# A 90-degree rotation of an 8192 x 8192 matrix: a third output buffer, five chunks fewer, and the last tile kept whole

## The chip, the core and the metric

The kernel runs on one core of one Trainium2 chip. The metric is the time of one execution in microseconds (us). Each kernel was executed several times, in turn with the kernel before on the same chip. All the times below are of runs that the records call fast.

The engines in the profiles are these. PE is the matrix engine, and PEld is its loading of the stationary operand. DVE is VectorE, ACT is ScalarE, and POOL is GpSimd. SP is the engine whose queue issues the loads. Every transfer runs on the 16 DMA engines of the core.

## The reference

```python
def setup_inputs():
    return {"x": np.random.randn(8192, 8192).astype(np.float32), "k": 1}

def reference(x, k):
    return np.rot90(x, k)          # out[i, j] = x[j, 8191 - i]
```

All 268.44 MB are read once and written once. The rest is rearrangement.

## The kernel before

The matrix is cut into 16 macro tiles of 1024 rows x 4096 columns. A macro tile is loaded as eight row tiles of 128 x 4096 (2 MiB each, one load each). VectorE copies each row tile into eight "chunks" of 128 x 512 and reverses the columns within each block of 128. PE then transposes the 128 x 128 blocks into PSUM, ScalarE copies the PSUM tile to an output buffer, and one store of 2 MiB writes four blocks of output rows. A macro tile has eight such outputs, and each needs a block from every one of its row tiles.

```python
    a_pool = ctx.enter_context(tc.tile_pool(name="a_pool", bufs=2))    # loads, 2 MiB each
    r_pool = ctx.enter_context(tc.tile_pool(name="r_pool", bufs=68))   # chunks; 64 hold a macro tile
    o_pool = ctx.enter_context(tc.tile_pool(name="o_pool", bufs=2))    # outputs, 2 MiB each
    psum_pool = ...  bufs=2
    ...
            for h in range(0, G, PW):                 # an output has two PSUM tiles
                pt = psum_pool.tile([P, FP], mybir.dt.float32, tag="ps")
                for w in range(PW):                   # column by column ...
                    g = g0 + h + w
                    for t in range(rt):               # ... through all row tiles
                        nc.tensor.transpose(..., chunks[t, g * P // CH][:, g % (CH // P), :], ident)
                nc.scalar.copy(o[:, G - PW - h : G - h, :], ps)
                ...
                    nc.scalar.dma_start(out=dst, in_=o[:, G - done : G - done + S, :])
    ...
    *most, before_last, last = tiles       # the last macro tile is split into 4 + 4 row tiles
    for m in most:
        store(*m, load(*m), False)
    c1 = load(*before_last)
    c2 = load(*last)
    store(*before_last, c1, True)
    store(*last, c2, True)                 # the very last output is stored in two halves
```

Of the kernel before, what the change touches and what calls it, by code (L numbers as in the profile page):

```python
# [2 lines left out]

# [5 lines left out]

P = 128  # L10




R = 1024
RT = R // P
LAST = [4, 4]
W = 4096
CH = 512
F = 4096  # L20
FP = 2048


def whole_reads(nc):






    for fn in nc.m.functions:
        for block in fn.blocks:
            for n, ins in enumerate(block.instructions):
                if not isinstance(ins, mybir.InstDMACopy):
                    continue
                src = ins.ins[0]
                ap = [list(d) for d in src.ap]
                if len(ap) == 3 and ap[2][0] == 1 and ap[1][0] == ap[2][1]:
                    ap = [ap[0], [1, 1], [1, ap[1][1] * ap[2][1]]]
                    block.instructions[n] = copy.replace(  # L40
                        ins,
                        ins=[copy.replace(src, ap=ap)],
                        ant_dge_precooked=False,
                    )


def macro_tiles(N, M):

    tiles = [(r0, RT, c0) for r0 in range(0, N, R) for c0 in range(0, M, W)]
    r0, _, c0 = tiles.pop()  # L50
    for n in LAST:
        tiles.append((r0, n, c0))
        r0 += n * P
    return tiles


@with_exitstack
def kernel(
    ctx: ExitStack,
    tc: tile.TileContext,  # L60
    x: bass.AP,
    k: bass.AP,
    out: bass.AP,
):
    nc = tc.nc
    assert k == 1, f"only k=1 supported, got {k}"
    nc.at_finalize(whole_reads)

    N, M = x.shape
    dt = x.dtype  # L70

    consts = ctx.enter_context(tc.tile_pool(name="consts", bufs=1))
    ident = consts.tile([P, P], dt)
    make_identity(nc, ident)

    a_pool = ctx.enter_context(tc.tile_pool(name="a_pool", bufs=2))
    r_pool = ctx.enter_context(tc.tile_pool(name="r_pool", bufs=68))
    o_pool = ctx.enter_context(tc.tile_pool(name="o_pool", bufs=2))
    psum_pool = ctx.enter_context(
        tc.tile_pool(name="psum", bufs=2, space=bass.MemoryType.PSUM)  # L80
    )

    loads = 0

    def load(r0, rt, c0):





        nonlocal loads
        chunks = {}
        for t in range(rt):


            if loads < RT and loads % 4 >= 2:
                a = o_pool.tile([P, W], dt, tag="o")
            else:
                a = a_pool.tile([P, W], dt, tag="a")
            loads += 1  # L100
            nc.sync.dma_start(
                out=a[:], in_=x[r0 + t * P : r0 + (t + 1) * P, c0 : c0 + W]
            )
            for j in range(W // CH):
                ar = r_pool.tile([P, CH // P, P], dt, tag="ar")
                nc.vector.tensor_copy(  # L106
                    out=ar[:],
                    in_=a[:, j * CH : (j + 1) * CH].rearrange(
                        "r (b m) -> r b m", m=P
                    )[:, :, ::-1],  # L110
                )
                chunks[t, j] = ar
        return chunks

    def store(r0, rt, c0, chunks, end):





        rows = rt * P
        PW = 1
        while 2 * PW * rows <= FP:
            PW *= 2
        G = PW
        while 2 * G * rows <= F:
            G *= 2
        for i, g0 in enumerate(range(0, W // P, G)):
            if end and i % 2 == 0:
                ot = a_pool.tile([P, F], dt, tag="a")  # L130
            else:
                ot = o_pool.tile([P, F], dt, tag="o")
            o = ot[:, : G * rows].rearrange("m (g f) -> m g f", g=G)

            S = PW if end and r0 + rows == N and g0 + G == W // P else G
            for h in range(0, G, PW):
                pt = psum_pool.tile([P, FP], mybir.dt.float32, tag="ps")
                ps = pt[:, : PW * rows].rearrange("m (g f) -> m g f", g=PW)
                for w in range(PW):
                    g = g0 + h + w  # L140
                    for t in range(rt):
                        nc.tensor.transpose(  # L142
                            ps[:, PW - 1 - w, t * P : (t + 1) * P],
                            chunks[t, g * P // CH][:, g % (CH // P), :],
                            ident,
                        )
                nc.scalar.copy(o[:, G - PW - h : G - h, :], ps)  # L147

                done = h + PW
                if done % S == 0:  # L150
                    top = M - c0 - (g0 + done) * P
                    dst = out[top : top + S * P, r0 : r0 + rows].rearrange(
                        "(g m) f -> m g f", g=S
                    )
                    nc.scalar.dma_start(  # L155
                        out=dst, in_=o[:, G - done : G - done + S, :]
                    )

    tiles = macro_tiles(N, M)
    *most, before_last, last = tiles  # L160
    for m in most:
        store(*m, load(*m), False)

    c1 = load(*before_last)
    c2 = load(*last)
    store(*before_last, c1, True)
    store(*last, c2, True)


# [1 line left out]
_INS = ['x', 'k']  # L171
_OUTS = [((8192, 8192), 'float32')]

_NUMBERS = {'k': 1}


# [26 lines left out]
```

## Time and profile before

| | before |
|---|---|
| median, lowest, highest of the first 3 runs | 1267.77, 1267.59, 1268.42 us |
| span of the profiled execution | 1266.0 us |
| bytes read + written | 268.44 + 268.44 MB, 424 GB/s over the span |
| busy: PE, ACT, DVE | 55%, 37%, 28% |
| DMA share in the 40 slices | 9 tenths in 39 of them |

The DMA row and the GB/s row decide here. The DMA engines are at nine tenths or more in nearly every slice, so the other engines only have to keep them fed. The lines themselves stand in the prediction. The column "DMA share" of the stage tables is the mean over 16 engines.

### The profile page before, as it was taken

What the parts mean: (1) busy time and instruction counts of PE and PEld (TensorE: products, weight loads), DVE (VectorE), ACT (ScalarE), POOL (GpSimd) and SP (SyncE); (2) the same over time, 40 slices, a digit from 0 to 9 for tenths busy, and PEclk for the clock granted to TensorE, in tenths of its full rate; (3) what the DMA queues carried; (4) which work ended last, traced back from release to release, by engine and by line L of the source; (5) the groups of instructions that cost most, each with busy time, mean ns of one, the idle gap of its engine ahead of it and who ended that gap; (6) DMA issues with size and microseconds to landing.
All of it is one profiled execution on the core that took longest, in us unless ns stands there. A gap on an engine that the chain in (4) does not pass through costs nothing.

```text
span 1266.0 us, 10386 instructions
## 1 busy us (share of the span) xinstructions
PE 700.4 (55%) x4096; PEld 660.8 (52%) x4096; DVE 354.9 (28%) x1024; ACT 467.3 (37%) x257; POOL 0.7 (0%) x6
## 2 busy tenths in 40 slices
PE   1456455665655555555556546565464665656573
PEld 0355455554545455554555445464464654556573
DVE  4422322232222322233222322233222332223210
ACT  0333334333433334333433334333433334333364
POOL 0000000000000000000000000000000000000000
PEclk9986777777678777787777877778777667777687
DMA  9999999999999999999999999999999999999998
GB/s 398 416 431 429 429 428 429 430 427 430 427 429 429 429 429 430 428 429 428 430 428 428 429 429 427 427 429 426 430 429 427 414 428 430 426 427 428 428 393 370
DMA packets 37057, 537.55 MB, mean 425 GB/s; under 512 B 4112, under 2 KB 4112, under 8 KB 4112
## 3 DMA queue, kind: packets, MB, share of 16 engines
q10 hardware_dynamic: 18576, 268.44, 50.0%
q1 hardware_dynamic: 18432, 268.44, 49.9%
q8 instruction: 32, 0.52, 0.2%
q14 instruction: 17, 0.14, 0.0%
HBM read 268.44 MB, written 268.44 MB: 424 GB/s over the span
## 4 chain that ended last, share of the span: by engine, by line
DMA 78%; ACT 19%; issue 1%; DVE 1%; ACTq 0%; PE 0%; DVEq 0%
DMA out_dram<-ot 74%; ACT ot L147 19%; DMA a<-in_x_dram 3%; DVE ar L106 1%; ACTq L155 0%; PE pt L142 0%; ACTq L147 0%; DVEq L106 0%
## 5 line engine op out<-in xcount | busy, mean ns | idle before, releaser
L142 PE MATMUL pt<-ident,ar 128*128 128x128 f32 x4096 | 700.4, 350 | 548.3 <-ACT ot L147 465.9
L142 PEld LDWEIGHTS pt<-ident,ar 128*128 128x128 f32 x4096 | 660.8, 187 | 587.7 <-ACT ot L147 496.4
L147 ACT COPY ot<-pt 128x2048 f32<-128x2048 f32 x256 | 466.0, 1869 | 742.6 <-DMA out_dram<-ot 729.5
L106 DVE COPY ar<-a 128x512 f32<-128x512 f32 x1024 | 354.9, 420 | 865.8 <-DMA a<-in_x_dram 811.4
L147 ACT ACT_TABLE_LOAD x1 | 1.3, 1283 | 41.1 <-DVE ar L106 41.1
masks.py:199 POOL TENSOR_SCALAR_AFFINE_SELECT ident<-ident 128x128 f32<-128x128 f32 x1 | 0.3, 294 | 0.1
masks.py:197 POOL MEMSET ident<- 128x128 f32 x1 | 0.2, 205 | 0.3 <-POOLq L184 0.3
L184 POOL MEMSET const-bfloat16-1.0<- 128x1 bf16 x1 | 0.1, 102 | 0.0
L184 POOL MEMSET const-uint8-127<- 128x1 uint8 x1 | 0.1, 102 | 0.0
L184 POOL MEMSET const-float32-0.0<- 128x1 f32 x1 | 0.1, 99 | 0.2 <-issue 0.2
L184 POOL MEMSET const-float32-1.0<- 128x1 f32 x1 | 0.1, 99 | 0.0
## 6 DMA issues: line engine op xcount, KB each, us to landing
a<-in_x_dram SPq DMA_DIRECT2D x128, 2048.0 KB, 16.8
out_dram<-ot ACTq DMA_DIRECT2D x127, 2048.0 KB, 15.9
out_dram<-ot ACTq DMA_DIRECT2D x2, 1024.0 KB, 13.7
```

The lines of the kernel that those rows point to most:

```text
L106: nc.vector.tensor_copy(out=ar[:], in_=a[:, j * CH : (j + 1) * CH].rearrange("r (b m) -> r b m", m=P)[:, :, ::-1],)
L142: nc.tensor.transpose(ps[:, PW - 1 - w, t * P : (t + 1) * P], chunks[t, g * P // CH][:, g % (CH // P), :], ident,)
L147: nc.scalar.copy(o[:, G - PW - h : G - h, :], ps)
L184: nc = _bacc.Bacc("TRN2", target_bir_lowering=False, num_devices=1)
```

## The change

The change is meant to keep the store queue filled. A third output buffer lets three stores be in flight; to make room for it, the chunks go from 68 to 63. The first output of each macro tile is transposed row tile by row tile, so that its chunks come free as the rows arrive. The last macro tile is no longer split. Its first output, like its last one, is stored in two halves. One line of the change is left out below: at the start the first eight loads are spread over five buffers (`loads % 5`) where they were spread over four, since the new output buffer is lent to them too.

```diff
-LAST = [4, 4]
...
-    tiles = [(r0, RT, c0) for r0 in range(0, N, R) for c0 in range(0, M, W)]
-    r0, _, c0 = tiles.pop()
-    for n in LAST:
-        tiles.append((r0, n, c0))
-        r0 += n * P
-    return tiles
+    return [(r0, RT, c0) for r0 in range(0, N, R) for c0 in range(0, M, W)]
...
-    r_pool = ctx.enter_context(tc.tile_pool(name="r_pool", bufs=68))
-    o_pool = ctx.enter_context(tc.tile_pool(name="o_pool", bufs=2))
+    r_pool = ctx.enter_context(tc.tile_pool(name="r_pool", bufs=63))
+    o_pool = ctx.enter_context(tc.tile_pool(name="o_pool", bufs=3))
...
-            S = PW if end and r0 + rows == N and g0 + G == W // P else G
+            S = PW if end and (i == 0 or g0 + G == W // P) else G
...
+            if i == 0 and (rt == RT or r0 + rows < N):
+                for h in range(G // PW):
+                    psum_tile(h)
+                for t in range(rt):
+                    transposes(t, range(G))
             for h in range(0, G, PW):
-                (transposes column by column, as above)
+                if h // PW not in ps:
+                    psum_tile(h // PW)
+                    (transposes column by column, as before)
...
-    c1 = load(*before_last)
-    c2 = load(*last)
-    store(*before_last, c1, True)
-    store(*last, c2, True)
+    for m in tiles:
+        store(*m, load(*m), m == tiles[-1])
```

## The prediction

> **What bounds the kernel now.** I read four views in this order: the page's slices, the page's groups, a table of stages, and the timeline at the two ends. The page first.
>
> ```profile
> PEclk9986777777678777787777877778777667777687
> DMA  9999999999999999999999999999999999999998
> GB/s 398 416 431 429 429 428 429 430 427 430 427 429 429 429 429 430 428 429 428 430 428 428 429 429 427 427 429 426 430 429 427 414 428 430 426 427 428 428 393 370
> HBM read 268.44 MB, written 268.44 MB: 424 GB/s over the span
> L142 PE MATMUL pt<-ident,ar 128*128 128x128 f32 x4096 | 700.4, 350 | 548.3 <-ACT ot L147 465.9
> L147 ACT COPY ot<-pt 128x2048 f32<-128x2048 f32 x256 | 466.0, 1869 | 742.6 <-DMA out_dram<-ot 729.5
> L106 DVE COPY ar<-a 128x512 f32<-128x512 f32 x1024 | 354.9, 420 | 865.8 <-DMA a<-in_x_dram 811.4
> ```
>
> The DMA row is 9 in every slice but the last. The rate is 426 to 431 GB/s in nearly all slices, and lower only in the first two, in one late slice (414) and in the last two. ScalarE waits 729.5 of its 742.6 idle us for stores, VectorE 811.4 of 865.8 for loads, and PE for ScalarE. So everything waits in the end for the DMA engines, and every byte must go through them: the output needs all of the input, 268.44 MB each way. The chain of waits says the same: 74% stores, 19% ScalarE copies, 3% loads. Its 19% should not be read as a fifth of the span to be won: a store lands, its buffer is refilled in 3.64 us and stored again, but the other buffer's store and two loads run beside that copy.
>
> What one transfer costs is best read where nothing but loads runs, in the timeline of the first 50 us:
>
> ```profile
> 12.99 2.77 DVE L106 COPY ar<-a 128x512 f32<-128x512 f32 x8 [2.12 <-DMA a<-in_x_dram]
> 17.88 2.77 DVE L106 COPY ar<-a 128x512 f32<-128x512 f32 x8 [2.12 <-DMA a<-in_x_dram]
> 22.79 2.77 DVE L106 COPY ar<-a 128x512 f32<-128x512 f32 x8 [2.13 <-DMA a<-in_x_dram]
> ```
>
> VectorE starts on each load as it lands, so loads of 2 MiB land 4.90 us apart: 2.097 MB / 4.90 us = 428 GB/s, the same rate as in the mixed middle. There are 128 loads and 128 stores' worth of data, so the data alone takes 256 x 4.90 = 1253 us (1254 if the page's mean middle rate of 428 is used). The time of 1267.8 is thus 14 us above what the engines need, 1.1%, and that is the whole purse for a change that moves no byte less. The table of stages says where it lies:
>
> ```profile
> core 0: us, PE busy (x) PEld busy (x) DVE busy (x) ACT busy (x) POOL busy (x), PEclk, DMA share, GB/s
> 0.00:3.00 3.00, 0.00 (x0) 0.00 (x0) 0.00 (x0) 0.00 (x0) 0.70 (x6) 1.00 0.44 104
> 3.00:76.00 73.00, 25.23 (x141) 21.31 (x142) 30.50 (x88) 15.93 (x9) 0.00 (x0) 0.93 1.01 424
> 76.00:1204.00 1128.00, 637.45 (x3670) 604.13 (x3669) 318.87 (x920) 417.01 (x230) 0.00 (x0) 0.74 1.01 428
> 1204.00:1222.00 18.00, 14.54 (x91) 14.02 (x92) 5.55 (x16) 9.41 (x6) 0.00 (x0) 0.74 0.88 371
> 1222.00:1262.00 40.00, 23.21 (x200) 21.31 (x198) 0.00 (x0) 24.91 (x14) 0.00 (x0) 0.86 1.00 418
> 1262.00:1266.00 4.00, 0.00 (x0) 0.00 (x0) 0.00 (x0) 0.00 (x0) 0.00 (x0) 0.50 0.11 47
> ```
>
> The last two columns are what counts. I turn each rate into time lost against 428: start 3 x (1 - 104/428) = 2.3 us; loads and first stores 73 x (1 - 424/428) = 0.7; middle 0; a hole near the end 18 x (1 - 371/428) = 2.4; the stores alone 40 x (1 - 418/428) = 0.9; after the last byte 4 x (1 - 47/428) = 3.6. The sum is 9.9; the rest of the 14 us is 1.8 us by which the timed run is longer than the profiled span, the DMA of instructions (0.66 MB, 1.5 us), and rounding.
>
> **The hole**, seen closely in the timeline and in 2-us windows:
>
> ```profile
> 1211.80 3.63 ACT L147 COPY ot<-pt 128x2048 f32<-128x2048 f32 x2 [6.21 <-DMA out_dram<-ot]
> 1215.46 0.55 ACTq L155 DMA_DIRECT2D out_dram<-ot  x1
> 1220.82 0.55 ACTq L155 DMA_DIRECT2D out_dram<-ot  x1
> ...
> 1214.00:1216.00 2.00, 2.00 (x11) 2.00 (x11) 0.00 (x0) 1.43 (x1) 0.00 (x0) 0.50 0.29 123
> 1220.00:1222.00 2.00, 2.00 (x21) 1.96 (x20) 0.76 (x3) 1.33 (x2) 0.00 (x0) 1.00 0.66 279
> ```
>
> No load is left to issue after 1201 us. The last store of the second-last macro tile waits until a buffer is stored (1211.7), is copied in 3.63 us and issued at 1215.46. Meanwhile only one store and the rest of the last load are in the queues; they run dry at about 1214 (share 0.29). The next store is issued 5.4 us later, while one store is 4.9 us of work, and there is a second hole (0.66).
>
> **What the Trainium skill says.** (1) "DMA: Bandwidth & Descriptors", Where 436 GB/s comes from: the 16 ports give 435.2 GB/s. The trace's 428 in the middle is 98% of that, so it agrees, and leaves no room for a faster middle. (2) The same page, Queues, rings and completion order: each DMA engine takes turns between the queue rows that have work, packet by packet. The trace agrees: the two queues took 50.0% and 49.9% of the engines' time. It follows that a deeper store queue doesn't take bandwidth from loads, it only keeps its own turn filled. (3) The same page, Latency and other measured facts: a fixed cost of about 2 us per DMA, mostly the receipt from memory. The first load landed 7.33 us after issue and carries 4.90 us of data, so 2.4 us here; this is why a single outstanding store isn't enough at the end.
>
> **The change, part by part.**
>
> Work on the engines: unchanged. 4096 transposes, 1024 reversals, 256 copies, 128 loads stay; stores go from 127 of 2048 KB and 2 halves to 126 and 4 halves. One more issue of 0.55 us on ScalarE's queue: nothing.
>
> Third output buffer: a copy waits for the store three back, not two back. Stores in flight rise from 15.9/9.8 = 1.6 to about 2.6 (9.8 us is the time for one load and one store). In the middle the engines are full already: gain 0.
>
> 63 chunks, 68 before: a chunk is 128x512 floats; 64 hold a macro tile. With 68, after output i of a tile is transposed, 8i + 12 chunks of the next can be filled; row tile i needs 8i + 8, so it is complete after output i. With 63 it is 8i + 7, so it is complete only after output i + 1. But with three buffers output i + 1 is transposed once output i is evicted, which waits for store i - 3; before, output i was transposed once output i - 1 was evicted, which waited for the same store i - 3. Loads keep their place against the stores that have landed: cost 0. The 64th chunk needs one chunk of its own macro tile free. That is what the row-by-row first output is for: row tile 0's four transposes release its first chunk before row tile 7 is reversed, so it can't deadlock. After the last row tile only 4 transposes are left to do in place of up to 18 or so, and the first store goes out about 1.5 us earlier (49.65 us before). At the start this is worth nothing, since two more loads fill the engines at that moment.
>
> The end: the last load should land with the rest of one store and two whole stores queued, some 2.6 x 4.9 = 12 us of work. Until the first new half store is issued it takes a reversal 0.42, four transposes about 0.7, a copy 1.87: 3.0 us, and some 0.6 us of issue. 12 against 3.6: no hole. After that an output costs ScalarE 4.3 us (issue to issue 1225.13 to 1229.46) against 4.9 us of transfer, and five buffers alternate: it stays filled. Gain: 2.4 us.
>
> The last macro tile whole: its stores write rows of 1024 floats instead of 512. Whether the 418 GB/s of the store-only stretch comes from the short rows or from stores alone the trace doesn't say; I take half of the 0.9 us: 0.5. Against that, the store-only stretch is longer by about one store.
>
> Start 2.3 and after the last byte 3.6: untouched. Sum: 2.4 + 0.5 = 2.9 us, so 1267.8 - 2.9 = **1264.9 us**.
>
> **Rivals.** (a) The deeper queue speeds the middle. For: the page's rate dips, such as 414 in one slice. Against: share 1.01 and 98% of the ceiling; even 430 in place of 428 over 1128 us would give only 5 us more: about 1260. (b) The chunk limit becomes the wait. For: VectorE already waited seven times, 54.4 us in total, for PE to release chunks, and there are now five chunks fewer. If loads lose step at each of 16 macro tiles for 2 us with the stores drained, it is +30 us, 1295. Against: the counting above, and three stores to fill in. (c) PSUM: the first output now holds both PSUM tiles while row tiles arrive. But PE and ScalarE have nothing else to do then; it would need all outputs of the tile before to be held, and they are evicted already. Zero, 1265. (d) The hole merely moves: 1268.
>
> **Range and chances.** Low end: all of hole and store-only stretch recovered and a little in the middle, 1261.5. High end: nothing recovered, 1268. Two per cent faster is 1242, below the 1253 of data alone: impossible at this rate, so 0.01 for a surprise in the rate. Slower by 2% is rival (b): 0.01.
>
> **What would show it.** Right: middle at 428 again; no 2-us window between the last load and the last store under 0.9 of DMA share; stores landing in about 25 us in place of 15.9; the store-only stretch about 50 us. Wrong: VectorE's waits for PE growing by tens of us with DMA share under 0.95 in the middle (b); a middle rate above 430 (a); a hole at the last load with a DMA share of 0.3 as now (d).

## The result

| | before | changed |
|---|---|---|
| median, lowest, highest of 6 runs each | 1268.09, 1267.59, 1269.21 us | 1269.88, 1269.54, 1270.63 us |
| ratio to before, 95% interval | | 1.0014, 1.0002 to 1.0027 |
| span of the profiled execution | 1266.0 us | 1268.8 us |

A ratio here is the mean time of one kernel's fast runs over the mean of the other's of the same rounds, so it is not quite the ratio of the medians. The changed kernel is within 2% of the old one, as forecast, but it is 1.8 us slower where 2.9 us faster was predicted.

The page of the changed kernel: the rate in 40 slices, ScalarE's copies with what they waited for, and the stores with their median time from issue to landing.

```profile
GB/s 398 427 429 430 429 428 429 429 429 429 428 429 427 430 429 428 428 429 429 429 428 429 430 420 430 429 429 427 424 430 428 417 429 426 427 428 424 429 338 381
L158 ACT COPY ot<-pt 128x2048 f32<-128x2048 f32 x256 | 466.4, 1869 | 762.3 <-DMA out_dram<-ot 506.5
out_dram<-ot ACTq DMA_DIRECT2D x126, 2048.0 KB, 25.5
```

Stores now take 25.5 us from issue to landing, where they took 15.9: three are in flight, as intended. ScalarE waits less for stores (506.5 us, before 729.5). The middle has the rate that it had. The slice before the last fell from 393 to 338 GB/s; the last has 381 in place of 370.

The stages of the changed kernel, cut as in the prediction (columns as there; the last two are DMA share and GB/s):

```profile
3.00:76.00 73.00, 30.16 (x177) 25.96 (x178) 30.62 (x88) 19.46 (x11) 0.00 (x0) 0.96 1.01 429
76.00:1204.00 1128.00, 625.40 (x3665) 587.76 (x3663) 319.14 (x920) 417.25 (x230) 0.00 (x0) 0.74 1.01 428
1204.00:1222.00 18.00, 8.13 (x36) 7.19 (x37) 5.55 (x16) 4.45 (x3) 0.00 (x0) 0.59 0.85 359
1222.00:1262.00 40.00, 28.18 (x222) 26.33 (x220) 0.00 (x0) 26.48 (x15) 0.00 (x0) 0.88 0.92 385
```

The middle is 428 GB/s in both. By this mean, all of the loss is after 1204 us: 359 in place of 371, and 385 in place of 418.

The end in the timeline of the changed kernel (start, duration, engine, work, count, and in brackets the idle time before it and what ended it):

```profile
1202.12 3.63 ACT L158 COPY ot<-pt 128x2048 f32<-128x2048 f32 x2 [6.19 <-DMA out_dram<-ot]
1205.78 0.55 ACTq L166 DMA_DIRECT2D out_dram<-ot  x1
...
1218.09 2.77 DVE L100 COPY ar<-a 128x512 f32<-128x512 f32 x8 [7.03 <-DMA a<-in_x_dram]
...
1219.30 3.63 ACT L158 COPY ot<-pt 128x2048 f32<-128x2048 f32 x2 [13.55 <-PE pt L137]
1221.19 2.31 ACTq L166 DMA_DIRECT2D out_dram<-ot  x2
...
1221.22 8.32 PE L137 MATMUL pt<-ident,ar 128*128 128x128 f32 x48 [1.53 <-ACT ot L158]
...
1227.84 1.87 ACT L158 COPY ot<-pt 128x2048 f32<-128x2048 f32 x1 [1.04 <-PE pt L137]
1229.73 0.55 ACTq L166 DMA_DIRECT2D out_dram<-ot  x1
```

The same stretch in windows of 2 us of the changed kernel:

```profile
1218.00:1220.00 2.00, 1.12 (x4) 0.72 (x4) 1.91 (x6) 0.70 (x1) 0.00 (x0) 0.50 0.50 213
1220.00:1222.00 2.00, 0.78 (x4) 0.78 (x5) 0.86 (x3) 2.00 (x2) 0.00 (x0) 0.50 0.14 57
...
1228.00:1230.00 2.00, 1.79 (x17) 1.55 (x15) 0.00 (x0) 1.70 (x1) 0.00 (x0) 1.00 0.08 29
1230.00:1232.00 2.00, 1.72 (x16) 1.48 (x14) 0.00 (x0) 1.60 (x1) 0.00 (x0) 1.00 0.61 262
```

**The first hole.** The last store of the tile before the last is issued at 1205.78. ScalarE then waits 13.55 us for PE, because the first output of a whole last tile needs its eighth row tile, which lands at 1218.09. In those 12.3 us the DMA engines can move 12.3 x 428 GB/s = 5.3 MB, or 2.5 transfers. From 1218 us on the rate falls to 213 and then 57 GB/s: for most of the DMA engines nothing is left to do.

**The second hole.** The first output is stored in two halves at 1221.19, which is 4.9 us of transfer. The next store follows only at 1229.73. PE was idle from 1210 to 1218.6 us, and its granted clock, the third column from the right, is 0.50. The 48 transposes that start at 1221.22 (32 for the second output, 16 for the third) take 8.32 us, and the copy waits for them.

### The profile page after: what moved, and what is told of

Its sections match the earlier page's. It is cut to its first block, busy times and chain, and to the rows that moved or that the text cites. A ratio compares the mean times of both kernels' runs of the same rounds, so it can differ in the third digit from the quotient of the medians.

```text
span 1268.8 us, 10386 instructions
## 1 busy us (share of the span) xinstructions
PE 691.9 (55%) x4096; PEld 647.2 (51%) x4096; DVE 355.3 (28%) x1024; ACT 467.7 (37%) x257; POOL 0.7 (0%) x6
## 4 chain that ended last, share of the span: by engine, by line
DMA 80%; DVE 11%; ACT 4%; PE 3%; issue 1%; ACTq 0%; DVEq 0%; SPq 0%
DMA a<-in_x_dram 69%; DMA out_dram<-ot 11%; DVE ar L100 11%; ACT ot L158 4%; PE pt L137 3%; ACTq L166 0%; DVEq L100 0%; SPq L95 0%; ACTq L158 0%
## 5 line engine op out<-in xcount | busy, mean ns | idle before, releaser
L137 PE MATMUL pt<-ident,ar 128*128 128x128 f32 x4096 | 691.9, 347 | 561.4 <-ACT ot L158 401.5
L137 PEld LDWEIGHTS pt<-ident,ar 128*128 128x128 f32 x4096 | 647.2, 184 | 605.8 <-ACT ot L158 438.2
L158 ACT COPY ot<-pt 128x2048 f32<-128x2048 f32 x256 | 466.4, 1869 | 762.3 <-DMA out_dram<-ot 506.5
## 6 DMA issues: line engine op xcount, KB each, us to landing
out_dram<-ot ACTq DMA_DIRECT2D x126, 2048.0 KB, 25.5
```

The costliest lines, as they stand in the source:

```text
L137: nc.tensor.transpose(ps[w // PW][:, PW - 1 - w % PW, t * P : (t + 1) * P], chunks[t, g * P // CH][:, g % (CH // P), :], ident,)
L158: nc.scalar.copy(o[:, G - PW - h : G - h, :], ps[h // PW])
```

## The experiments

### A second way of reading the end: the last landing

The first experiments gave results that the mean DMA share could not explain, so I read one more thing from the traces. Each transfer marks its landing 16 times, once for each DMA engine. The Trainium skill says so ("DMA: Bandwidth & Descriptors", Why a DMA increments its semaphore by 16 and not by 1), and the trace agrees: the kernel before has 257 transfers and 4112 landing records, 16 x 257. A transfer is complete with the sixteenth. The sixteen are far apart. In the kernel before, first and last mark of one transfer are 2.2 us apart at the start (median of the first 32 transfers), 7.1 us in the fourth 32, and 8.2 to 8.4 in the fifth to seventh. So some DMA engines lag behind others by more than a transfer and a half (8.2 / 4.9). The next table, worked out from these records, has the time of the last mark for the end of eight runs.

```
us from the span's start; the last of 16 marks
                 last    last store    outputs of the last macro tile (a halved one: its second half)        from the 2nd   first-to-last
                 load    of the tile     1       2       3       4       5       6       7       8            column to      mark of the
                         before                                                                               output 8       last store
before          1217.9    1224.9      1229.9  1235.0  1240.1  1245.4  1250.1  1255.1  1260.0  1265.0         40.1           2.7
changed         1218.0    1224.8      1229.9  1236.5  1241.4  1246.4  1253.2  1258.0  1263.0  1267.8         43.0           2.0
e1_split_tail   1216.8    1224.0      1228.9  1233.9  1238.9  1243.9  1248.9  1253.9  1258.8  1263.8         39.8           7.0
e2_whole_tail.. 1218.3    1225.1      1231.0  1237.7  1242.6  1247.5  1253.6  1258.5  1263.4  1268.3         43.2           2.0
e4_warm_pe      1219.4    1225.5      1230.6  1235.6  1240.7  1246.8  1251.7  1256.6  1261.5  1266.4         40.9           1.8
r1_after        1219.7    1225.7      1230.8  1238.1  1243.0  1248.0  1254.8  1259.7  1264.6  1269.5         43.8           1.9
r2_warm         1217.5    1224.8      1229.7  1234.6  1240.3  1244.9  1249.8  1254.7  1259.7  1264.6         39.8           1.9
r3_split        1218.0    1225.0      1230.1  1235.1  1240.1  1245.2  1250.1  1255.1  1260.0  1265.0         40.0           7.1
```

Two things can be read here. In the kernel before, stores complete every 5 us from 1224.9 to the end, straight through the "hole" that the mean showed there. And the last store of the tile before the last completes at the same time before and after the change (1224.9 and 1224.8): nothing up to there made a difference, not even the first hole of the changed kernel, since output 1 also completes at 1229.9 in both. A caution: each row is one execution. Those of e1_split_tail, e4_warm_pe and r2_warm are the fastest of their kernels (r2_warm's took 1267.37 us, its others 1269.20 to 1269.86), that of the changed kernel is its slowest. So the distances within a row say more than the times at which it ends.

### e1_split_tail: the old end with the rest of the change

```diff
-    return [(r0, RT, c0) for r0 in range(0, N, R) for c0 in range(0, M, W)]
+    (split of the last macro tile into 4 + 4, both loaded before either is stored, as before)
-            S = PW if end and (i == 0 or g0 + G == W // P) else G
+            S = PW if end and r0 + rows == N and g0 + G == W // P else G
```

> The changed kernel with only its end put back: last macro tile split 4+4, both halves loaded before either is stored, only the very last output in halves. Theory A (the whole last macro tile has nothing to store between the last store of the tile before it and its own eighth row tile, so the store queue runs dry while the last load is under way): no 2-us window under 0.9 of DMA share between 1204 us and the end, and about 1265 us, 3 us under the kernel before and 5 under the changed one. Rival B (the third output buffer or the chunk limit costs the time): stays at about 1270 us, with the middle under 428 GB/s.

Measured: 1267.69 us median of 5 (1266.55 to 1268.63), ratio to before 1.0001 (0.9987 to 1.0014). Three profiles of one 30-us stretch follow: before, changed, and this one.

```profile
1210.00:1240.00 30.00, 24.22 (x197) 22.42 (x195) 3.65 (x11) 23.11 (x13) 0.00 (x0) 0.94 0.93 389
```

```profile
1210.00:1240.00 30.00, 18.78 (x133) 17.33 (x132) 3.83 (x12) 15.60 (x9) 0.00 (x0) 0.77 0.80 334
```

```profile
1210.00:1240.00 30.00, 22.78 (x197) 20.98 (x194) 2.77 (x8) 22.48 (x13) 0.00 (x0) 1.00 1.01 421
```

The hole is gone, as theory A (in the expectation above) said: 421 GB/s where the kernel before has 389. By the mean that is 30 x (421 - 389)/428 = 2.2 us won. Yet the time is that of the kernel before, not 1265. What the engines gained on average they lost at the end of the same run:

```profile
1256.00:1258.00 2.00, 0.00 (x0) 0.00 (x0) 0.00 (x0) 0.00 (x0) 0.00 (x0) 0.50 0.70 291
1258.00:1260.00 2.00, 0.00 (x0) 0.00 (x0) 0.00 (x0) 0.00 (x0) 0.00 (x0) 0.50 0.47 197
```

The DMA share falls step by step, as one engine after another runs out of work, while the last goes on to 1263.8: the marks of the last store are 7.0 us apart (2.7 before). That is why I formed theory D: the end is set by the DMA engine that lags most, and a hole in the mean makes the leading engines wait, not the lagging one. Theory A holds for the difference to the changed kernel. Rival B (third buffer or chunk limit) falls, since both are in this run. So is the new start.

### e2_whole_tail_only: the new end with the rest as before

The edit is the reverse: the kernel before with only the hunks of the end (no split, first and last output in halves).

> The kernel before (two output buffers, 68 chunks, transposes column by column) with only the end of the change: last macro tile whole, its first output stored in halves. Theory A: slower than before by 1.5 to 4 us, 1269.5 to 1272 us, with holes after the last load lands at about 1218 us. Rival B: 1268 us or less, since neither the third buffer nor 63 chunks are in it.

Measured: 1271.14 us (1269.42 to 1271.38), ratio 1.0022 (1.0009 to 1.0034), within the 1269.5 to 1272 expected. The end alone makes the kernel slower, by about as much as the whole change does. Rival B fails a second time.

### e3_column_order: without the row-by-row order

```diff
-            if i == 0 and (rt == RT or r0 + rows < N):
+            if False:
```

> The changed kernel without the row-by-row order of the first outputs. Theory A: after the last row tile lands, 9 transposes in place of 2 or 4 stand before the first copy, at some 0.19 us each with the lower granted clock: the first hole grows by 1 to 1.5 us and the time to about 1271 us; the middle stays at 428 GB/s. Rival C (the row-by-row order itself costs time, by holding both PSUM tiles while rows arrive): faster than the changed kernel, 1268 us or less.

Measured: 1275.09 us (1274.12 to 1276.83), ratio 1.0058 (1.0045 to 1.0070). It is slower than the changed kernel as expected, but by about 5 us, and not in the place expected: the middle suffers. The table of stages of this run in windows of 20 us:

```profile
900.00:920.00 20.00, 11.81 (x89) 10.97 (x89) 5.64 (x16) 7.59 (x5) 0.00 (x0) 0.77 1.00 406
...
960.00:980.00 20.00, 7.13 (x39) 6.20 (x39) 5.55 (x16) 6.10 (x4) 0.00 (x0) 0.68 1.01 431
980.00:1000.00 20.00, 12.91 (x89) 12.15 (x89) 5.64 (x16) 7.89 (x5) 0.00 (x0) 0.72 0.99 394
```

From about 510 us on, about once per macro tile (some 78 us), the rate of a window dips to about 400 GB/s; over 76 to 1204 us it is 426 in place of 428, which is 1128 x 2/428 = 5 us. Why there are no such dips before wasn't looked into. With 63 chunks, the 64th of a macro tile waits until the first output is transposed. In column order that output can only be transposed after the eighth row tile arrives, and the freed load buffer comes late each time. The last load lands at 1223.2 us by its last mark, against 1218.0 in the changed kernel. So the row-by-row order pays for the missing five chunks, and costs nothing that these runs show. Rival C falls.

### e4_warm_pe and r2_warm: PE kept busy before the second hole

```diff
                 for t in range(rt):
+                    if end and t == rt - 1:
+                        for _ in range(72):      # overwritten by the right ones
+                            nc.tensor.transpose(ps[0][:, PW - 1, t * P : (t + 1) * P],
+                                                chunks[t - 1, 0][:, 0, :], ident)
                     transposes(t, range(G))
```

> The changed kernel with 72 needless transposes on PE between row tile 6 and row tile 7 of the last macro tile's first output (overwritten by the right ones). If the second hole (1226 to 1231 us) comes from PE working at 0.5 of its clock after idling, PE shows 1.0 there, the second output's 32 transposes take 3.5 us in place of 6.6, the second hole shrinks by about 3 us, and the time is about 1267 us. If the second hole has another cause (ScalarE or the store queue), the time stays at 1270 us.

Measured: 1269.86 us (1269.18 to 1272.18), ratio 1.0019 (1.0006 to 1.0031): the time expected if the clock had nothing to do with it. But the profile did what was asked: 32 transposes of the second output in 3.74 us at a clock of 1.0, and outputs 1 and 2 completed 5.0 us apart in place of 6.6. The changed kernel had been timed in other rounds, so I ran the pair again side by side on one chip, with the split end (r3_split, the same edit as e1_split_tail) as third.

> The changed kernel once more, beside the next two on one chip, for a comparison without a change of chip. About 1270 us, some 2 us over the kernel before. Reading by the last landing of each store on the 16 DMA engines: the last store of the tile before the last lands at 1224 to 1226 us as before the change; then eight stores take 43 us, with one gap of 6.5 us or more at the second output.

> The changed kernel with the 72 needless transposes again. If the second hole costs what the last landings of the profiles say (5.0 us between the first and second output in place of 6.6), it is 1 to 2 us faster than the changed kernel of the same rounds. If it is the same within 0.5 us, the second hole costs nothing in the time and the extra time lies elsewhere.

Measured: the changed kernel 1272.25 us (1269.14 to 1272.45), ratio 1.0024 (1.0011 to 1.0038), some 2 us more than expected; with PE kept busy 1269.27 us (1267.37 to 1269.86), ratio 1.0005 (0.9991 to 1.0019). The two profiles, first the changed kernel, then the one with PE kept busy: transposes after the first output, and the issue of the second output's store.

```profile
1222.92 8.25 PE L137 MATMUL pt<-ident,ar 128*128 128x128 f32 x48 [1.53 <-ACT ot L158]
...
1231.36 0.55 ACTq L166 DMA_DIRECT2D out_dram<-ot  x1
```

```profile
1220.43 3.74 PE L138 MATMUL pt<-ident,ar 128*128 128x128 f32 x32 [1.74 <-ACT ot L166]
...
1226.49 0.55 ACTq L174 DMA_DIRECT2D out_dram<-ot  x1
```

From the start of those transposes to the store it is 8.4 us in the first and 6.1 in the second. Outputs 1 and 2 complete 7.3 us apart in the first, 4.9 in the second. Side by side the medians are 3.0 us apart, with one of the five runs of the changed kernel as fast as the other kernel. In this comparison the half clock is most of the loss, more than the 1 to 2 us expected. e4_warm_pe, set against the first timing of the changed kernel, shows no such gain, so over both pairs it isn't settled how much the half clock costs: the mean of the two ratios is 1.0019 without and 1.0012 with the warm PE, and each interval is about 0.0025 wide.

> The changed kernel with the old split end again. Theory A: 1.5 to 3 us faster than the changed kernel of the same rounds, and the same as the kernel before within 0.7 us (theory D: filling the hole that the mean shows is worth nothing). Rival M: 2.4 us faster than the kernel before.

Measured: 1267.83 us (1267.19 to 1268.21), ratio 0.9996 (0.9983 to 1.0008). That is 4.4 us under the changed kernel of the same rounds by the medians, more than expected, and the same as the kernel before, as theory D says. Rival M asks for 2.4 us under the kernel before, a ratio of 0.9981, which is just outside this interval and outside the one of e1_split_tail.

### p8_pause and p14_pause: a hole on purpose

```diff
-                nc.scalar.copy(o[:, G - PW - h : G - h, :], ps)
+                pause = 8 if (r0, c0, i, h) == (4 * R, 0, 3, 0) else 0     # 14 in p14_pause
+                for _ in range(1 + pause):
+                    nc.scalar.copy(o[:, G - PW - h : G - h, :], ps)
```

> The kernel before with a hole made on purpose in the middle: one copy of one output (macro tile 8, output 3) is done nine times, so that its store goes out 8 x 1.87 = 15 us late. Measured in the windows around it, the hole should be 3 to 7 us of the 16 engines' mean time. Theory D (the end is set by the DMA engine that lags most; the landings of one transfer on the 16 engines are 7 to 8 us apart in the middle, the mean engine some 5 to 6 us ahead of the last; a hole in the mean up to that size only makes the leading engines wait): the time rises by 0 to 2 us, and the spread of landings drops right after the pause. Rival M (a hole costs what the mean DMA share loses, as the prediction reckoned): the time rises by the whole hole, 3 to 7 us.

Measured: 1281.36 us (1280.94 to 1281.71, 4 runs), ratio 1.0103. The pause was not the one planned: in the timeline ScalarE's extra copies are dealt out over more than one output, and the stores go out at 693.93, 717.26, 734.50, 736.33 and 754.84 us, where 9.8 us lie between two otherwise. The hole in this run:

```profile
700.00:720.00 20.00, 9.80 (x48) 8.66 (x48) 6.99 (x20) 17.39 (x10) 0.00 (x0) 0.62 0.90 358
720.00:740.00 20.00, 7.96 (x48) 7.33 (x48) 4.21 (x12) 8.27 (x5) 0.00 (x0) 0.61 0.62 213
```

With 424 and 398 GB/s in the 20-us windows at 680 and 760 us, the mean lost 3.3 + 10.0 + 0.2 + 1.4 = 14.9 us against 428. The time rose by 13.0 us (difference of the means). The distance of the marks fell from 7.2 us (median of the fourth 32 transfers) to 4.2 and 2.5 us in the next two. So some of the hole was given back, but only 1.9 us. Theory D had put 4 to 6 us on that, rival M none. The direction is D's, the size is not. The last landings split this further: the last store of the tile before the last is 11.9 us late (1236.8 in place of 1224.9), so 3.0 us of the hole had been given back by then. The outputs of the last macro tile then took 41.9 us in place of 40.1, with the DMA engines level (0.2 us apart) where that tile begins.

> The same with fifteen copies, the store 26 us late, hole in the mean some 12 to 18 us. Theory D: the time rises by the hole less 4 to 6 us. Rival M: by the whole hole.

Measured: 1371.55 us, 103 us more. This run tells nothing about holes. The extra copies changed the order of ScalarE's program after the pause: a copy of the next output now stands ahead of each store's issue, and the rate stays at about 340 to 390 GB/s until the end.

### i32_pool and i64_pool: more instructions to fetch

Why do some DMA engines lag? The page lists 32 packets of 16 KB and 17 of 8 KB for instructions. In the changed kernel, one such fetch at 1250.2 us took 0.93 us, and three data packets around it took 0.90, 0.93 and 1.01 us, where the median is 0.61: about 1.9 us more for one engine if all four were on the same one. The trace names no engine, but each of the four starts within 0.01 us of the end of the one before, as packets of one engine would. Output 5 of that run completes 6.8 us after output 4, and the distance of the marks goes from 0.3 to 2.1 us there. These runs add instructions that no engine waits for:

```diff
         for i, g0 in enumerate(range(0, W // P, G)):
+            for _ in range(32):                      # 64 in i64_pool
+                nc.gpsimd.memset(spare[:], 0.0)      # one column, never read
```

> The kernel before with 4096 memsets of one column on the idle POOL engine (0.1 us each, nothing waits for them): 0.26 MB more instructions to fetch through the DMA engines. Theory F (each fetch of 16 KB holds up a single DMA engine by about 2 us, as at 1250 us of the changed kernel, and this makes some engines lag): 16 more fetches, 32 us of engine time, 2 us if they fall evenly on 16 engines, up to 10 if on few; the spread of landings grows faster. Rival: 0.26 MB is 0.6 us at 428 GB/s, no more.

Measured: 1277.72 us (1276.88 to 1278.57), ratio 1.0073: 9.3 us more by the means, for bytes worth 0.6 us, so the rival's figure falls. First and last mark of a transfer are 7.1 us apart already in the second 32 transfers, where the kernel before has 2.7: the engines do drift apart faster, as theory F said. The rate while POOL has instructions left, and after:

```profile
100.00:700.00 600.00, 347.93 (x1920) 330.25 (x1920) 166.53 (x480) 218.11 (x120) 411.27 (x3274) 0.74 1.01 423
800.00:1200.00 400.00, 231.27 (x1312) 219.32 (x1312) 113.80 (x328) 149.04 (x82) 0.00 (x0) 0.76 1.01 428
```

> The same with 8192 memsets, 0.52 MB, 32 more fetches. Theory F: 4 us if even, up to 20 if on few engines. Rival: 1.2 us.

Measured: 1473.07 us, but only because POOL itself needed that long; I had misjudged its pace, so the time is void. The last landing is still of use: 1285.3 us, against 1275.0 in i32_pool and 1265.0 before, so about 10 us for each 4096 instructions. That is the upper end of what theory F allowed for the smaller dose. The fetches came in 32 more packets of 8 KB per dose, at 0.31 us each for those of the kernel before: 32 x 0.31 = 9.9 us, what a single engine would lose if it served them all. The traces don't name the engine of a packet, so this fits but isn't shown, and another effect of POOL's memsets is not excluded.

### The changed kernel again

r1_after, told above beside r2_warm, is the second timing of the changed kernel: ratio 1.0024 after 1.0014.

## Why the prediction was wrong

**What was right.** The bound is the DMA engines, and no part of the change touches the middle: 428 GB/s before and after (rival a falls). The counting of buffers held: 63 chunks with three buffers cost nothing (e1_split_tail 1.0001, r3_split 0.9996), and VectorE's waits for PE grew only from 54.4 to 77.9 us. Stores take 25.5 us to land, where about 25 was expected. The first store goes out at 48.04 us in place of 49.65 and is worth nothing: the mean of the first stage rose from 424 to 429 GB/s, but the last store before the end completes at the same time. The whole last tile's stores give about what was guessed, 0.5 us: without a hole they complete 4.9 us apart, those of the split one 5.0, some 0.1 us for each of eight. That this comes from the longer rows was not tested alone. Holding both PSUM tiles costs nothing (rival c).

**The step that failed first** reads: "the last load should land with the rest of one store and two whole stores queued, some 2.6 x 4.9 = 12 us of work". It landed with the rest of one store queued (its 16 marks run from 1218.2 to 1224.8) and no whole store behind it: none of the two. I had taken the mean number of stores in flight, and assumed that the last store of the tile before would be issued at about the time when the last load lands. The trace shows 12.3 us between them. The profile of before had the number, in these two lines:

```profile
1205.62 0.55 ACTq L155 DMA_DIRECT2D out_dram<-ot  x1
1217.98 2.78 DVE L106 COPY ar<-a 128x512 f32<-128x512 f32 x8 [7.11 <-DMA a<-in_x_dram]
```

The last load lands at 1217.98, and the next-to-last store of that tile is issued at 1205.62. One more buffer moves the last store into that place, 12.4 us before the last load lands, and nothing follows, since a whole tile can't store anything until its eighth row tile is there. The split had existed to prevent just this. That it is the end that got worse shows in both directions: e2_whole_tail_only makes the old kernel slower, e1_split_tail and r3_split make the changed one as fast as the old.

**The second failed step** is the term "a hole near the end 18 x (1 - 371/428) = 2.4", booked as a gain. Even a filled hole was worth nothing: e1_split_tail and r3_split fill it and stay level with the kernel before. The DMA share is a mean of 16 engines; the last landings come every 5 us through the hole, so the engines that lag lost nothing in it. For the same reason the first hole of the changed kernel, 18 x (1 - 359/428) = 2.9 us in the mean, cost nothing either: its output 1 completes at 1229.9 us, as before.

**What made it slower** is the second hole, which the prediction ruled out with the words "After that an output costs ScalarE 4.3 us (issue to issue 1225.13 to 1229.46) against 4.9 us of transfer". From the second half of output 1 (issued at 1222.96) to output 2 (1229.73) it was 6.8 us. The prediction reckoned "four transposes about 0.7" us, which is what a PE kept busy needs (0.66 in r2_warm; here they took 1.12), and didn't ask what clock the 32 transposes of the second output would have. The Trainium skill warns of it ("TensorE: Matmul & The Clock Gate", Why this matters for your kernels: PE idle for more than about 3 us falls back to the lower clock). The trace agrees: idle from 1210 to 1218.6 us, granted clock 0.50, and 48 transposes in 8.32 us (0.21 us from one to the next up to 1227.0, then 0.11), where a PE kept busy does 32 in 3.74. Outputs 1 and 2 complete 6.6 us apart instead of 5.0: 1.6 us. A second late step, 6.8 us from output 4 to output 5, adds 1.8. The closer stores of the whole tile give back some 0.7, which leaves 1.6 + 1.8 - 0.7 = 2.7 of the 2.8 us by which the profiled spans differ.

The first of these late steps is confirmed by r2_warm in its own round, though not by e4_warm_pe. The second stands beside an instruction fetch and hits engines that the holes had just brought level. The 16 marks show it: those of output 4 lie within 0.3 us, of those of output 5 fifteen lie within 0.4 us and the sixteenth comes 1.7 us after them. So one engine fell behind. r1_after has the same (fetch at 1251.79 us, 6.8 us to the next last mark, one late engine), and e2_whole_tail_only and e3_column_order nearly so (fetches at 1250.60 and 1254.82, 6.1 us). In e1_split_tail and r3_split, whose engines are 7 us apart, two such fetches fall in the last macro tile too, and no step is over 5.1 us. That the fetch is the cause, and that engines far apart hide it, fits all six profiles but was not tested by an edit.

**A slip, and the range.** 256 x 4.90 is 1254.4, not 1253, so the purse was 13 us, not 14; nothing hangs on it. The range ended at 1268 because the worst case was "nothing recovered". Rival (d), "The hole merely moves", came nearest, but gave the hole no room to grow. Rival (b), the chunk limit, doesn't happen in this kernel, but e3_column_order shows how close it was: without the row-by-row order it costs 5 us. I had also called that order the thing that prevents a deadlock. It isn't: e3_column_order runs without it and is correct.

No version tried beats the kernel before clearly: e1_split_tail, at 1.0001, and r3_split, at 0.9996, are the same.

## What to carry to other kernels

Deepen a queue only together with the question of what will be left to put into it: at the end of a kernel, list for each store the last load that it needs, and keep something storable until the last load has landed. A small hole in the mean share of 16 DMA engines is not yet lost time (a large one is: of 14.9 us in p8_pause, 13.0 were lost); look at the last of the 16 landings of each transfer, and count only the gaps there. And after a wait of several microseconds, time PE's next work at the lower clock.

## What the Trainium skill lacked or had wrong

- No page says how far the DMA engines of a core drift apart under a plain stream of loads and stores. Here first and last landing of one transfer are 2.2 us apart in the first 32 transfers and 8.2 to 8.4 in the fifth to seventh. "DMA: Bandwidth & Descriptors", Latency and other measured facts, does say that two engines are usually slower, and guesses at the descriptor rings of GpSimd's queue; these kernels issue no transfer from GpSimd and drift all the same. The traces name no engine, so whether the same two lag here is open.
- "Runtime: NRT & Kernel Launch", Instruction fetch mechanics, says that instructions are fetched by DMA and that the cost is mostly hidden; it doesn't say that the fetches may hold up data transfers. Here 4096 more POOL instructions (0.26 MB) cost 9.3 us, 15 times what their bytes need at 428 GB/s. Whether the fetches alone cost that, and whether through one engine, is open.
